# Token-major projections of 512 columns, transposed afterwards by pairs of heads, in a two-layer hybrid encoder

## The chip, the cores and the metric

The kernel runs on one core of a Trainium2 chip. The metric is device time in microseconds (us) of one execution, as the median of several runs. The core's engines work side by side, each through its own instruction list in order: TensorE (PE in the profile; its weight loads stand apart as PEld), VectorE (DVE), ScalarE (ACT), GpSimd (POOL), and the queue of SyncE (SP), which here only issues DMAs.

## The reference

The input is 256 tokens of 2048 features. Two pre-norm residual layers follow each other, then a last RMSNorm.

- Layer 0 (even) projects the normalised tokens with one matrix into eight query heads, two key heads and two value heads of branch A (grouped-query attention, RMS-normalised q and k, rotary positions), into q, k, v of branch B (eight heads of differential attention with a distance bias: two softmaxes over 64-wide halves, the second subtracted with a learned factor, then a norm per head), and into a gate of 2048 columns.
- Layer 1 (odd) projects into q, k, v and gate of sixteen heads (branch C). Its three dilated windows are merged by their softmax denominators, which for 256 tokens is one softmax with a bias and a mask.

```
proj = einsum('bsd,de->bse', rms_norm(h, g), w_in)
y    = concat(attention outputs) * silu(gate)
h    = h + einsum('bse,ed->bsd', y, w_out)
```

Inputs and outputs are float32.

## The kernel before

Every large product is done in a split form. A weight group of 1024 columns by 128 rows is loaded as `raw` (512 KB, SP's queue, four buffers), ACT copies it to `hi` (rounded to fp32r), DVE subtracts to get `lo`; activations are held as such a pair too. A product is hi·hi + hi·lo + lo·hi, three passes of TensorE. Both split instructions are issued with high priority (lines 160, 161), so each projection carries, beside its matmuls, one ACT and one DVE instruction of 1024 columns per group.

A projection of the 256 tokens is one of two kinds of job:

- `job_t` (lines 168 to 170, through `mm3`) is token-major: the stationary operand is 128 tokens of the activations, the moving one 512 weight columns. 512 output columns take 2 token tiles x 16 feature tiles x 3 passes = 96 matmuls of 512 columns. Its result has tokens on the partitions.
- `job_e` (lines 199, 200) is feature-major: the stationary operand is 128 weight columns, the moving one is hi and lo of all 256 tokens, 512 columns wide, for the weight's `hi`, and hi alone, 256 wide, for its `lo`. 256 output columns take 2 x 16 pairs of such matmuls, 64 in all. Its result has features on the partitions, as attention wants q and k; ACT and DVE then add its two halves (lines 203, 204).

Before, A's q, k and v, every v and the output projections are `job_t`; all gates, B's q and k, and C's q and k are `job_e`: 16 jobs of 256 columns in the even layer, 24 in the odd one. A's q and k, token-major because of their norm and rotation, are turned by four transposes of 128x128 per pair of heads (`zt`, line 527). A norm factor per token that a feature-major result needs along its free axis is made by `token_stats` with a diagonal and four small matmuls (`bps`, line 240), once per layer.

A head's attention is: scores (6 matmuls of 256 columns, in B 8, into a PSUM tile `bank`), a bias on DVE, row maximum on DVE, exponential on ACT, scaling on ACT, four transposes of the softmax (line 346), a split of those, the values' product (6 matmuls of 256 columns), the gate. Branch B then transposes the result for its norm (line 417), takes a power on POOL (line 221) and spreads the factor over the partitions with two more matmuls (`rb`, line 421).

The order of each engine's list is set at compile time by the framework's scheduler, which goes through the program in the order in which it is written and lets later matmuls pass where earlier ones are not ready by its own estimate. On the chip each engine keeps that list. There are four PSUM tiles `acc` (two per job) and four `att` (attention, `zt`, `bps`).

Of the kernel before, what the change touches and what calls it, by code (L numbers as in the profile page):

```python
# [17 lines left out]
P = 128  # L18
# [46 lines left out]
def job_columns(name):  # L65

    if name == "even":
        cols = [(A_KV0, 512)]
        for g in range(4):
            c = g * 256  # L70
            cols += [(c, 512)] * (g % 2 == 0) + [(GATE_E + c, 256), (GATE_E + 1024 + c, 256), (B_Q0 + c, 256), (B_K0 + c, 256)]
            cols += [(B_V0 + c, 512)] * (g % 2 == 0)
        return cols
    if name == "odd":
        cols = []
        for g in range(8):
            c = g * 256
            cols += [(3 * D + c, 256), (c, 256)]
            if g % 2 == 0:
                cols.append((2 * D + c, 512))  # L80
            cols.append((D + c, 256))
        return cols
    return list(CHUNKS_E if name == "out_even" else CHUNKS)
# [19 lines left out]
def trunk(ctx, tc, x, xt, w_even, w_oe, w_odd, w_oo, gain_cols, rows, final_g, rope_c, geo_c, out):  # L103
# [81 lines left out]
    def job_e(w, c0, wd, a):  # L185


        kn = 1024 // wd
        ps = [acc.tile([P, 512], F32, tag="acc", name=f"acc_e{b}") for b in range(wd // P)]
        for kg in range(NK // kn):  # L190
            hi, lo = wgroup(w, c0, wd, kg)
            for b in range(wd // P):
                for kk in range(kn):
                    k = kg * kn + kk
                    bs = slice(b * P, (b + 1) * P)
                    whole = (ps[b], hi[:, kk, bs], a[k].rearrange("p i s -> p (i s)"))
                    half = (ps[b][:, :S], lo[:, kk, bs], a[k][:, 0])
                    first, second = (whole, half) if k == 0 else (half, whole)
# [6 lines left out]
        return [e[:, b] for b in range(2)]  # L205

# [21 lines left out]
    def token_stats(parts, scale):  # L228

        ss = small.tile([P, NT], F32, tag="ss", name="ss")  # L230
        V.reduce_sum(ss, parts, axis=AX.X)
        rstd = small.tile([P, NT], F32, tag="rstd", name="rstd", bufs=2)
        V.tensor_copy(rstd, rsqrt_mean(ss, D, NORM_EPS, NT))
        rs = small.tile([P, NT], F32, tag="rs", name="rs", bufs=2)
        V.tensor_scalar_mul(rs, rstd, scale)
        ps = att.tile([P, 512], F32, tag="att", name="bps")
        for t in range(NT):
            diag = work.tile([P, S], F32, tag="yf", name="diag")[:, :P]
            V.tensor_scalar_mul(diag, ident, rstd[:, t:t + 1])
            T.matmul(ps[:, t * P:(t + 1) * P], ones, diag, start=True, stop=True)  # L240
        bc = heads.tile([P, S], F32, tag="bc", name="bc", bufs=1)
        V.tensor_copy(bc, ps[:, :S])
        return rstd, rs, bc
# [6 lines left out]
    def evac_q(ps, n=2):  # L250
        t = heads.tile([P, 2, 2, S], F32R, tag="q", name="q", bufs=2)
        for b in range(n):
            split(t[:, b, 0], t[:, b, 1], ps[b])
        return t

    def evac_k(ps, bc):
        t = heads.tile([P, 2, 2, S], F32R, tag="k", name="k", bufs=2)
        kf = work.tile([P, 2, S], F32, tag="kf", name="kf")
        for b in range(2):
            V.tensor_mul(kf[:, b], ps[b], bc)  # L260
        split(t[:, :, 0], t[:, :, 1], kf)
        return t
# [3 lines left out]
    def evac_q64(ps):  # L266
        t = heads.tile([P, 2, 2, S], F32R, tag="q", name="q", bufs=2)
        for b in range(2):
            for j in range(2):
                js, other = slice(64 * j, 64 * j + 64), slice(64 - 64 * j, 128 - 64 * j)  # L270
                A.activation(t[js, b, j], ps[b][js], AF.Copy)
                V.tensor_sub(t[other, b, j], ps[b][js], f(t[js, b, j]))
        return t

    def evac_k64(ps, bc):
        kh = heads.tile([P, 2, 2, S], F32R, tag="k", name="kh", bufs=2)
        kl = heads.tile([P, 2, 2, S], F32R, tag="k", name="kl", bufs=2)
        kf = work.tile([P, 2, S], F32, tag="kf", name="kf")
        for b in range(2):
            V.tensor_mul(kf[:, b], ps[b], bc)  # L280
        for j in range(2):
            js, other = slice(64 * j, 64 * j + 64), slice(64 - 64 * j, 128 - 64 * j)
            A.activation(kh[js, :, j], kf[js], AF.Copy)
            A.activation(kh[other, :, j], kf[js], AF.Copy)
            V.tensor_sub(kl[js, :, j], kf[js], f(kh[js, :, j]))
            A.activation(kl[other, :, j], f(kl[js, :, j]), AF.Copy)
# [12 lines left out]

    def evac_gate(ps, bc):  # L300

        gt = heads.tile([P, 2, S], F32, tag="gate", name="gate", bufs=2)
        for b in range(2):
            V.tensor_mul(gt[:, b], ps[b], bc)
        e = work.tile([P, 2, S], F32, tag="e", name="e", bufs=1)
        A.activation(e, gt, AF.Exp, scale=-1.0)
        V.tensor_scalar_add(e, e, 1.0)
        for b in range(2):
            for c in range(0, S, S // 4):
                V.reciprocal(e[:, b, c:c + S // 4], e[:, b, c:c + S // 4])  # L310
        V.tensor_mul(gt, gt, e)
        return gt
# [62 lines left out]
    def biased(sp, rs, bias):  # L375
        s = stile()
        for t in range(NT):
            V.scalar_tensor_tensor(s[:, t], sp[:, t], rs[:, t:t + 1], bias[:, t], op0=ALU.mult, op1=ALU.add)  # L378
        return s
# [8 lines left out]
    def head_b(h, i, q, kh, kl, v, vs, gate, rs):  # L388
        bias = alibi(2.0 ** -(i + 1), False)
        es, rd = [], []  # L390
        ps = [bank(), bank()]
        for j in range(2):
            for t in range(NT):
                o, qs = ps[j][:, t * S:(t + 1) * S], q[:, j, t * P:(t + 1) * P]
                T.matmul(o, qs, kh[:, j], start=t == 0, stop=False)  # L395
                T.matmul(o, qs, kl[:, j], start=False, stop=t == NT - 1)  # L396
            sp = ps[j].rearrange("p (t k) -> p t k", t=NT)
            s = biased(sp, rs, bias)
# [4 lines left out]
        for t in range(NT):  # L403
            A.activation(p[:, t], p[:, t], AF.Copy, scale=rd[0][:, t:t + 1])
            V.scalar_tensor_tensor(p[:, t], e2[:, t], rd[1][:, t:t + 1], p[:, t], op0=ALU.mult, op1=ALU.add)
        ph, pl = transposed(p, ps[0])
# [18 lines left out]
    def head_c(h, q, k, v, vs, gate, rs):  # L425
        bias = alibi(float(np.exp2(np.float32(-8.0 * (h + 1) / 16))), True)
        ps = bank()
        sp = scores(ps, q[:, 0], q[:, 1], k[:, 0], k[:, 1])
        p = biased(sp, rs, bias)
# [3 lines left out]
        weighted_v(h, p, v, vs, gate, ps)  # L433
# [64 lines left out]
    def tok_heads(ps, i, c0=0):  # L498

        z = work.tile([P, NT, 2 * HD], F32, tag="z", name="z", bufs=3)  # L500
        for t in range(NT):
            A.activation(z[:, t], ps[t][:, c0:c0 + 2 * HD], AF.Copy, scale=rstd[:, t:t + 1])
        sq = work.tile([P, 512], F32, tag="sq", name="sq", bufs=1)
        A.activation(sq, z.rearrange("p t c -> p (t c)"), AF.Square)
        ss = small.tile([P, 4], F32, tag="ss4", name="ss4")
        V.reduce_sum(ss, sq.rearrange("p (n e) -> p n e", e=HD), axis=AX.X)
        r = rsqrt_mean(ss, HD, NORM_EPS, 4, "ra")
        z3 = z.rearrange("p t (n e) -> p (t n) e", n=2)
        V.tensor_mul(z3, z3, r.unsqueeze(2).to_broadcast([P, 4, HD]))
        t2 = work.tile([P, NT, 2 * HD], F32, tag="t2", name="t2", bufs=1)  # L510
        for t in range(NT):
            s5 = z[:, t].rearrange("p (n s h e) -> p n s h e", n=2, s=2, h=2)
            o5 = t2[:, t].rearrange("p (n s h e) -> p n s h e", n=2, s=2, h=2)
            tab = rq[:, i, t, 1].rearrange("p (s h e) -> p s h e", s=2, h=2)
            for hh in range(2):
                V.tensor_mul(o5[:, :, :, hh], s5[:, :, :, 1 - hh],
                             tab[:, :, hh].unsqueeze(1).to_broadcast([P, 2, 2, 32]))
        z4 = z.rearrange("p t (n e) -> p t n e", n=2)
        V.tensor_mul(z4, z4, rq[:, i, :, 0].unsqueeze(2).to_broadcast([P, NT, 2, HD]))
        V.tensor_add(z, z, t2)  # L520
        return z

    def pair_t(z, tag):
        ps = att.tile([P, 512], F32, tag="att", name="zt")
        for j in range(2):
            for t in range(NT):
                T.transpose(ps[:, j * S + t * P:j * S + (t + 1) * P], z[:, t, j * HD:(j + 1) * HD], ident)
        dst = heads.tile([P, 2, 2, S], F32R, tag=tag, name=tag, bufs=1 if tag == "ka" else 2)
        split(dst[:, :, 0], dst[:, :, 1], ps.rearrange("p (j k) -> p j k", j=2))
        return dst  # L530

    rstd, rs_b, bc = token_stats(parts, 1.0 / math.sqrt(64))
# [137 lines left out]
```

## Time and profile before

| | before |
|---|---|
| median of 3 runs | 914.29 us (914.02 to 914.72) |
| profiled execution, time | 914.34 us |
| its span, first to last instruction | 912.6 us |
| PE busy | 901.6 us, 99% |
| DVE busy | 677.8 us, 74% |
| ACT busy | 528.6 us, 58% |
| mean granted TensorE clock | 0.998 of full speed |
| DMA, mean | 180 GB/s, 50.8% of 16 engines in the main queue |

Busy time of PE counts an instruction from its start to a modelled end, so neighbours overlap; what a matmul really takes of the engine is the distance from its start to the next one's. The chain is the work that ended last, followed back from the end, and tells by which engine and line the span was filled.

### The profile page before, as it was taken

To read this page: it belongs to the slowest core of one execution; us is meant where nothing else is said; L and a number is where in the kernel's file an instruction comes from. 1 tells how busy PE (TensorE), PEld (TensorE's weight loads), DVE (VectorE), ACT (ScalarE), POOL (GpSimd) and SP (SyncE) were. 2 spreads that over 40 slices of the span, in tenths; PEclk is the share of its full clock that TensorE was granted. 3 is DMA by queue.
4 is the path that set the end of the run, shared out by engine and by line. 5 is a ranking of instruction groups with operands and counts; after the bars stand their busy time and mean duration, and the time that the engine had idled before them with its cause. 6 is when DMAs were issued, how large, how long until landed. Compare 5 with 4: busy or idle time off the path is not lost.

```text
span 912.6 us, 13324 instructions
## 1 busy us (share of the span) xinstructions
PE 901.6 (99%) x4928; PEld 778.0 (85%) x4928; DVE 677.8 (74%) x1089; ACT 528.6 (58%) x909; POOL 87.0 (10%) x69
## 2 busy tenths in 40 slices
PE   9999999999999999999999999999999999999996
PEld 7888888888888887788888888888888888888886
DVE  6699788877979877656746886687758685776663
ACT  7756667575577666555445665465546464555551
POOL 0010010020200002000001120022003110202000
PEclk9999999999999999999999999999999999999999
DMA  8854544544544444455554445544454445456552
GB/s 327 316 211 150 186 171 151 175 162 162 191 159 177 145 178 165 138 190 186 179 195 170 170 161 188 186 164 167 174 191 160 181 166 184 162 185 215 188 192 95
DMA packets 47041, 164.46 MB, mean 180 GB/s; under 512 B 5376, under 2 KB 6144, under 8 KB 46976
## 3 DMA queue, kind: packets, MB, share of 16 engines
q1 hardware_dynamic: 46656, 162.57, 50.8%
q0 software_dynamic: 320, 1.05, 0.5%
q8 instruction: 38, 0.62, 0.3%
q14 instruction: 27, 0.22, 0.1%
HBM read 161.50 MB, written 2.10 MB: 179 GB/s over the span
## 4 chain that ended last, share of the span: by engine, by line
PE 96%; DVE 1%; DMA 1%; issue 1%; SPq 0%; ACT 0%; POOLq 0%; POOL 0%; DVEq 0%; ACTq 0%
PE acc_e L200 32%; PE acc_e L199 18%; PE acc_t L169 13%; PE acc_t L168 13%; PE acc_t L170 13%; PE bank L346 2%; PE bank L170 1%; PE bank L168 1%; PE bank L169 1%; DMA xk<-in_xt 1%; PE bank L326 1%; PE bank L325 1%; PE bank L324 1%; PE bank L396 0%; PE bank L395 0%
## 5 line engine op out<-in xcount | busy, mean ns | idle before, releaser
L161 DVE TENSOR_TENSOR lo<-raw,hi 128x1024 fp32r<-128x1024 f32 (+1 forms) x294 | 365.5, 1244 | 179.4 <-ACT hi L160 179.0
L160 ACT ACTIVATE hi<-raw 128x1024 fp32r<-128x1024 f32 (+1 forms) x294 | 309.6, 1054 | 285.8 <-PE acc_t L170 117.3
L200 PE MATMUL acc_e<-u,hi 128*128 128x512 f32 x1200 | 432.1, 399 | 0.0
L199 PE MATMUL acc_e<-u,lo 128*128 128x256 f32 x1200 | 338.5, 282 | 0.0
L200 PEld LDWEIGHTS acc_e<-u,hi 128*128 128x128 f32 x1200 | 225.4, 188 | 46.5
L199 PEld LDWEIGHTS acc_e<-u,lo 128*128 128x128 f32 x1200 | 226.7, 189 | 4.4
L169 PE MATMUL acc_t<-lo,u 128*128 128x512 f32 x288 | 111.7, 394 | 0.0
L170 PE MATMUL acc_t<-hi,u 128*128 128x512 f32 x288 | 110.7, 390 | 0.0
L168 PE MATMUL acc_t<-hi,u 128*128 128x512 f32 x288 | 102.7, 393 | 0.4 <-ACT u L214 0.4
L169 PE MATMUL acc_t<-lo,y 128*128 128x512 f32 (+1 forms) x256 | 96.6, 379 | 0.5 <-DVE lo L161 0.5
L383 POOL TENSOR_SCALAR bias<-geo 128x512 f32<-128x512 f32 x24 | 44.9, 1870 | 541.3 <-DVE s L378 520.4
L170 PE MATMUL acc_t<-hi,y 128*128 128x512 f32 (+1 forms) x256 | 95.2, 377 | 0.0
L168 PE MATMUL acc_t<-hi,y 128*128 128x512 f32 (+1 forms) x256 | 89.0, 379 | 0.6 <-ACT y L247 0.6
L169 PEld LDWEIGHTS acc_t<-lo,u 128*128 128x128 f32 x288 | 54.3, 189 | 11.3 <-DVE lo L161 0.4
L168 PEld LDWEIGHTS acc_t<-hi,u 128*128 128x128 f32 x288 | 53.8, 189 | 11.7 <-ACT u L214 1.1
L170 PEld LDWEIGHTS acc_t<-hi,u 128*128 128x128 f32 x288 | 54.2, 188 | 10.9
L310 DVE RECIPROCAL e<-e 128x64 f32<-128x64 f32 x128 | 56.3, 504 | 0.4
L169 PEld LDWEIGHTS acc_t<-lo,y 128*128 128x128 f32 x256 | 48.2, 188 | 9.5 <-DVE lo L161 1.0
L168 PEld LDWEIGHTS acc_t<-hi,y 128*128 128x128 f32 x256 | 47.7, 188 | 9.3 <-ACT y L247 0.8
L170 PEld LDWEIGHTS acc_t<-hi,y 128*128 128x128 f32 x256 | 48.2, 188 | 8.3
L203 ACT ACTIVATE sum<-acc_e 128x256 f32<-128x256 f32 x80 | 30.0, 375 | 20.3 <-PE acc_e L200 19.6
L204 DVE TENSOR_TENSOR sum<-acc_e,sum 128x256 f32<-128x256 f32 x80 | 33.2, 415 | 0.4 <-ACT sum L203 0.3
(155 smaller groups left out, 923.0 us busy)
## 6 DMA issues: line engine op xcount, KB each, us to landing
raw<-in_w_in_odd SPq DMA_DIRECT2D x128, 512.0 KB, 3.2
raw<-in_w_in_even SPq DMA_DIRECT2D x102, 512.0 KB, 3.2
raw<-in_w_out_even SPq DMA_DIRECT2D x32, 512.0 KB, 3.2
raw<-in_w_out_odd SPq DMA_DIRECT2D x32, 512.0 KB, 3.7
tok<-in_x SPq DMA_DIRECT2D x4, 512.0 KB, 8.6
xk<-in_xt SPq DMA_DIRECT2D x6, 256.0 KB, 6.9
raw<-in_w_in_even SPq DMA_DIRECT2D x4, 256.0 KB, 4.0
gf<-in_final_norm_g POOLq DMA_DIRECT2D x4, 256.0 KB, 4.4
```

What stands on the lines that cost most here:

```text
L160: A.activation(hi[:, ks], rv[:, ks], AF.Copy)
L161: splits.append(V.tensor_sub(lo[:, ks], rv[:, ks], f(hi[:, ks])))
L168: T.matmul(ps, ah, bh, start=start, stop=False)
L169: T.matmul(ps, ah, bl, start=False, stop=False)
L170: T.matmul(ps, al, bh, start=False, stop=stop)
L199: T.matmul(*first, start=k == 0, stop=False)
L200: T.matmul(*second, start=False, stop=k == NK - 1)
L203: A.activation(e[:, b], ps[b][:, S:], AF.Copy)
L204: V.tensor_add(e[:, b], ps[b][:, :S], e[:, b])
L310: V.reciprocal(e[:, b, c:c + S // 4], e[:, b, c:c + S // 4])
L346: T.transpose(ps[:, kt * S + t * P:kt * S + (t + 1) * P], p[:, t, kt * P:(kt + 1) * P], ident)
L383: G.tensor_scalar_mul(b, geo[:, 0], -slope)
```

## The change

All `job_e` are gone. The gates, B's q and k, and C's q and k become `job_t` of 512 columns, 20 in number, where 40 `job_e` of 256 stood. ACT evacuates each with the token's factor as a scale (`evac_t`); a gate becomes z·(1 + tanh z) with z half the projection (`gate_t`), in place of exponential, addition and reciprocal. Queries, keys and gates are then turned by pairs of heads: four transposes of 128x128 into one PSUM tile (`turned`), then the split or, for a gate, one copy. In each group of four heads the softmaxes come before the V projection and the values' products after it. `token_stats` loses its diagonal and its matmuls; the bias is added with one DVE instruction per head in place of two, the factor being in q and k already.

```diff
-    def job_e(w, c0, wd, a):
...
-                    T.matmul(*first, start=k == 0, stop=False)
-                    T.matmul(*second, start=False, stop=k == NK - 1)
-        e = work.tile([P, 2, S], F32, tag="kf", name="sum")
-        for b in range(2):
-            A.activation(e[:, b], ps[b][:, S:], AF.Copy)
-            V.tensor_add(e[:, b], ps[b][:, :S], e[:, b])
...
-            T.matmul(ps[:, t * P:(t + 1) * P], ones, diag, start=True, stop=True)
...
+    def evac_t(ps, r):
+        z = work.tile([P, NT, 512], F32, tag="z", name="z", bufs=3)
+        for t in range(NT):
+            A.activation(z[:, t], ps[t], AF.Copy, scale=r[:, t:t + 1])
+        return z
+    def gate_t(ps, rh):
+        z = evac_t(ps, rh)
+        for t in range(NT):
+            th = work.tile([P, 512], F32, tag="th", name="th", bufs=1)
+            A.activation(th, z[:, t], AF.Tanh)
+            V.scalar_tensor_tensor(z[:, t], th, 1.0, z[:, t], op0=ALU.add, op1=ALU.mult)
+        return z
+    def turned(z, pair):
+        ps = att.tile([P, 512], F32, tag="att", name="zt")
+        for j in range(2):
+            for t in range(NT):
+                c = (2 * pair + j) * HD
+                T.transpose(ps[:, j * S + t * P:j * S + (t + 1) * P], z[:, t, c:c + HD], ident)
+        return ps.rearrange("p (j k) -> p j k", j=2)
...
-        for b in range(2):
-            for c in range(0, S, S // 4):
-                V.reciprocal(e[:, b, c:c + S // 4], e[:, b, c:c + S // 4])
...
-        ps = job_e(w_odd, 3 * D + c, 256, u)
...
-        q = evac_q(job_e(w_odd, c, 256, u))
...
-        k = evac_k(job_e(w_odd, D + c, 256, u), bc)
-        for j in range(2):
-            head_c(2 * g + j, q[:, j], k[:, j], v[:, g % 2], slice(j * HD, j * HD + HD), gate[:, j], rs)
+        zg = gate_t(ps, rh)
+        zq = evac_t(job_t(w_odd, c, 512, u), rs)
+        zk = evac_t(job_t(w_odd, D + c, 512, u), rstd)
+        p = []
+        for pair in range(2):
+            q = pair_t(zq, pair, "q")
+            k = pair_t(zk, pair, "k")
+            p += [softmax_c(4 * g + 2 * pair + j, q[:, j], k[:, j]) for j in range(2)]
+        v = v_tile()
+        evac_v(v, job_t(w_odd, 2 * D + c, 512, u), rstd)
+        for pair in range(2):
+            gate = pair_gate(zg, pair)
+            for j in range(2):
+                weighted_v(4 * g + 2 * pair + j, p[2 * pair + j], v[:, pair], slice(j * HD, j * HD + HD), gate[:, j], bank())
```

On TensorE, in the middle of a projection of the odd layer, this stood before (`acc_e` is the PSUM tile of a `job_e`, `u,lo` and `u,hi` its activations with the weight part):

```order
L199 MATMUL acc_e_5060<-u,lo 128x256
L200 MATMUL acc_e_5060<-u,hi 128x512
L199 MATMUL acc_e_5060<-u,lo 128x256
L200 MATMUL acc_e_5060<-u,hi 128x512
L199 MATMUL acc_e_5060<-u,lo 128x256
```

In the changed kernel the V projection of the odd layer's second group reads like this (`acc_t` is the PSUM tile of a `job_t`; `zt` the tile of `turned`, here of a pair of keys):

```order
L159 MATMUL acc_t_5400<-hi,u 128x512 [waits Activation_49]
L159 MATMUL acc_t_5401<-hi,u 128x512
L234 MATMUL zt<-ident,z 128x128 [waits Activation_49]
L234 MATMUL zt<-ident,z 128x128 x2
L160 MATMUL acc_t_5400<-lo,u 128x512 [waits DVE_49]
L161 MATMUL acc_t_5400<-hi,u 128x512
L159 MATMUL acc_t_5400<-hi,u 128x512
```

Alternating widths have become one width, and transposes that wait for ACT's evacuation stand between the matmuls of the next job.

The second place is TensorE's list at the start of the even layer's output projection, where the last heads of branch B end. Before (`rb` spreads a head's norm factor; `y` is a head's finished output, the stationary operand of the output projection):

```order
L170 MATMUL acc_t_3872<-hi,y 128x512
L421 MATMUL bank<-ident,rb 128x128 [waits Pool_49]
L421 MATMUL bank<-ident,rb 128x128
L421 MATMUL bank<-ident,rb 128x128 [waits Activation_49,Pool_49]
L421 MATMUL bank<-ident,rb 128x128
L168 MATMUL acc_t_3699<-hi,y 128x512 [waits Activation_49]
L169 MATMUL acc_t_3699<-lo,y 128x512
```

In the changed kernel (`s` is a softmax; line 159 stands for 168, 392 for 421):

```order
L161 MATMUL bank<-ph,v 128x256
L392 MATMUL bank<-ident,rb 128x128 [waits Pool_49]
L392 MATMUL bank<-ident,rb 128x128
L392 MATMUL bank<-ident,rb 128x128 [waits Activation_49,Pool_49]
L392 MATMUL bank<-ident,rb 128x128
L159 MATMUL acc_t_3491<-hi,y 128x512 [waits Activation_49]
L159 MATMUL acc_t_3492<-hi,y 128x512
L315 MATMUL bank<-ident,s 128x128 [waits DVE_49]
L315 MATMUL bank<-ident,s 128x128 x3
L159 MATMUL acc_t_3319<-hi,y 128x512 [waits Activation_49]
```

Two heads ended there before; now four do, and two further sets of `rb` follow later in the same two output jobs.

## Rows read from the trace of the kernel before

**Rows 1.** The page: chain that ended last, by engine, then by line.

```profile
PE 96%; DVE 1%; DMA 1%; issue 1%; SPq 0%; ACT 0%; POOLq 0%; POOL 0%; DVEq 0%; ACTq 0%
PE acc_e L200 32%; PE acc_e L199 18%; PE acc_t L169 13%; PE acc_t L168 13%; PE acc_t L170 13%; PE bank L346 2%; PE bank L170 1%; PE bank L168 1%; PE bank L169 1%; DMA xk<-in_xt 1%; PE bank L326 1%; PE bank L325 1%; PE bank L324 1%; PE bank L396 0%; PE bank L395 0%
```

**Rows 2.** PE's waits in the span: us in total, times, longest.

```profile
PE acc_t L168 <- ACT y L247: 0.6, 1, 0.6
PE acc_t L169 <- DVE lo L161: 0.5, 1, 0.5
PE acc_t L168 <- ACT u L214: 0.4, 1, 0.4
PE bank L421 <- POOL rb L221: 0.2, 1, 0.2
```

**Rows 3.** Windows from job start to job start: length, PE busy (x instructions), clock, DMA.

```profile
450.53:472.29 21.76, 21.76 (x97) 1.00 0.62 216
472.29:483.59 11.30, 11.30 (x66) 1.00 0.53 188
```

**Rows 4.** Timeline, PE: start, length of one matmul; `job_e`, then `job_t`.

```profile
100.41 0.28 PE L199 MATMUL acc_e<-u,lo 128*128 128x256 f32 x1
100.52 0.40 PE L200 MATMUL acc_e<-u,hi 128*128 128x512 f32 x1
100.76 0.28 PE L199 MATMUL acc_e<-u,lo 128*128 128x256 f32 x1
101.93 0.40 PE L168 MATMUL acc_t<-hi,u 128*128 128x512 f32 x1
102.16 0.39 PE L169 MATMUL acc_t<-lo,u 128*128 128x512 f32 x1
```

**Rows 5.** Windows as in rows 3: jobs that hold attention matmuls or transposes.

```profile
483.59:496.32 12.73, 12.73 (x77) 1.00 0.49 177
496.32:508.05 11.73, 11.73 (x69) 1.00 0.39 137
508.05:521.06 13.01, 13.01 (x81) 1.00 0.54 190
63.05:76.15 13.10, 13.10 (x82) 1.00 0.48 162
472.29:569.28 96.99, 96.99 (x545) 1.00 0.49 174
```

**Rows 6.** Windows as in rows 3: `job_t` that hold attention matmuls or transposes.

```profile
29.17:51.43 22.26, 22.26 (x102) 1.00 0.75 271
403.99:426.64 22.65, 22.65 (x105) 1.00 0.54 187
545.51:569.28 23.77, 23.77 (x113) 1.00 0.54 191
```

**Rows 7.** Groups by line: busy us, mean ns of one, idle before.

```profile
L310 DVE RECIPROCAL e<-e 128x64 f32<-128x64 f32 x128 | 56.3, 504 | 0.4
L204 DVE TENSOR_TENSOR sum<-acc_e,sum 128x256 f32<-128x256 f32 x80 | 33.2, 415 | 0.4 <-ACT sum L203 0.3
L203 ACT ACTIVATE sum<-acc_e 128x256 f32<-128x256 f32 x80 | 30.0, 375 | 20.3 <-PE acc_e L200 19.6
L294 ACT ACTIVATE v<-acc_t,rstd 128x512 fp32r<-128x512 f32 x12 | 8.2, 681 | 3.2 <-PE acc_t L170 3.2
```

**Rows 8.** Timeline, DVE, then PE: A's first keys ready, then turned.

```profile
52.29 0.67 DVE L520 TENSOR_TENSOR z<-z,t 128x512 f32<-128x512 f32 x1
56.36 0.60 PE L527 MATMUL zt<-ident,z 128*128 128x128 f32 x4
```

**Rows 9.** Timeline, start of the even output projection: branch B's last norm.

```profile
370.43 0.27 PE L417 MATMUL bank<-ident,on 128*128 128x128 f32 x1
373.47 0.43 PE L421 MATMUL bank<-ident,rb 128*128 128x128 f32 x2 [0.23 <-POOL rb L221]
374.47 0.49 PE L168 MATMUL acc_t<-hi,y 128*128 128x512 f32 x1 [0.57 <-ACT y L247]
```

More of the change, by code (lines that the diff above doesn't have):

```diff
@@ L68, in job_columns @@
         cols = [(A_KV0, 512)]
[L69 to L72, printed above, removed]
+        for c in (0, 512):
+            cols += [(b + c, 512) for b in (0, GATE_E, GATE_E + 1024, B_Q0, B_K0, B_V0)]
         return cols
     if name == "odd":
[L75 to L82, printed above, removed]
+        return [(b * D + c, 512) for c in range(0, D, 512) for b in (3, 0, 1, 2)]
     return list(CHUNKS_E if name == "out_even" else CHUNKS)
@@ L231, in token_stats @@
         V.reduce_sum(ss, parts, axis=AX.X)
[L232 to L239, printed above, removed]
-            T.matmul(ps[:, t * P:(t + 1) * P], ones, diag, start=True, stop=True)
-        bc = heads.tile([P, S], F32, tag="bc", name="bc", bufs=1)
-        V.tensor_copy(bc, ps[:, :S])
-        return rstd, rs, bc
+        r3 = small.tile([P, 3, NT], F32, tag="rstd", name="rstd", bufs=2)
+        V.tensor_copy(r3[:, 0], rsqrt_mean(ss, D, NORM_EPS, NT))
+        V.tensor_scalar_mul(r3[:, 1], r3[:, 0], scale)
+        V.tensor_scalar_mul(r3[:, 2], r3[:, 0], 0.5)
+        return r3[:, 0], r3[:, 1], r3[:, 2]
     def split(hi, lo, src):
@@ new lines, in turned, with pair_t @@
+    def turned(z, pair):
[5 more added lines that the diff above has]
+        return ps.rearrange("p (j k) -> p j k", j=2)
+    def pair_t(z, pair, tag, bufs=2):
+        ps = turned(z, pair)
+        dst = heads.tile([P, 2, 2, S], F32R, tag=tag, name=tag, bufs=bufs)
+        split(dst[:, :, 0], dst[:, :, 1], ps)
+        return dst
@@ L251, in evac_q, with pair_gate, pair_q64 @@
+    def pair_gate(z, pair):
+        ps = turned(z, pair)
+        gt = heads.tile([P, 2, S], F32, tag="gate", name="gate", bufs=3)
+        A.copy(gt, ps)
+        return gt
+    def pair_q64(z, pair):
+        ps = turned(z, pair)
         t = heads.tile([P, 2, 2, S], F32R, tag="q", name="q", bufs=2)
-        for b in range(n):
-            split(t[:, b, 0], t[:, b, 1], ps[b])
-        return t
-    def evac_k(ps, bc):
-        t = heads.tile([P, 2, 2, S], F32R, tag="k", name="k", bufs=2)
-        kf = work.tile([P, 2, S], F32, tag="kf", name="kf")
-        for b in range(2):
-            V.tensor_mul(kf[:, b], ps[b], bc)
-        split(t[:, :, 0], t[:, :, 1], kf)
-        return t
@@ L266, in evac_q64 @@
-    def evac_q64(ps):
-        t = heads.tile([P, 2, 2, S], F32R, tag="q", name="q", bufs=2)
-        for b in range(2):
-            for j in range(2):
[L270 to L275, printed above, removed]
+        for j in range(2):
+            js, other = slice(64 * j, 64 * j + 64), slice(64 - 64 * j, 128 - 64 * j)
+            A.activation(t[js, :, j], ps[js], AF.Copy)
+            V.tensor_sub(t[other, :, j], ps[js], f(t[js, :, j]))
@@ L276, in evac_k64, with pair_k64 @@
+        return t
+    def pair_k64(z, pair):
+        ps = turned(z, pair)
         kh = heads.tile([P, 2, 2, S], F32R, tag="k", name="kh", bufs=2)
         kl = heads.tile([P, 2, 2, S], F32R, tag="k", name="kl", bufs=2)
-        kf = work.tile([P, 2, S], F32, tag="kf", name="kf")
-        for b in range(2):
-            V.tensor_mul(kf[:, b], ps[b], bc)
         for j in range(2):
             js, other = slice(64 * j, 64 * j + 64), slice(64 - 64 * j, 128 - 64 * j)
-            A.activation(kh[js, :, j], kf[js], AF.Copy)
-            A.activation(kh[other, :, j], kf[js], AF.Copy)
-            V.tensor_sub(kl[js, :, j], kf[js], f(kh[js, :, j]))
+            A.activation(kh[js, :, j], ps[js], AF.Copy)
+            A.activation(kh[other, :, j], ps[js], AF.Copy)
+            V.tensor_sub(kl[js, :, j], ps[js], f(kh[js, :, j]))
@@ L373, in head_a, with biased @@
         weighted_v(h, p, v, vs, gate, ps)
-    def biased(sp, rs, bias):
+    def biased(sp, bias):
         s = stile()
-        for t in range(NT):
-            V.scalar_tensor_tensor(s[:, t], sp[:, t], rs[:, t:t + 1], bias[:, t], op0=ALU.mult, op1=ALU.add)
+        V.tensor_add(s, sp, bias)
         return s
@@ L405, in head_b @@
             V.scalar_tensor_tensor(p[:, t], e2[:, t], rd[1][:, t:t + 1], p[:, t], op0=ALU.mult, op1=ALU.add)
+        return p
+    def head_b(h, p, v, vs, gate):
+        ps = [bank(), bank()]
         ph, pl = transposed(p, ps[0])
@@ L516, in tok_heads @@
                 V.tensor_mul(o5[:, :, :, hh], s5[:, :, :, 1 - hh],
[L517 to L520, printed above, removed]
-        return z
[L523 to L530, printed above, removed]
@@ L532, in trunk @@
-    rstd, rs_b, bc = token_stats(parts, 1.0 / math.sqrt(64))
+                             tab[:, :, hh].unsqueeze(1).to_broadcast([P, n, 2, 32]))
+            V.tensor_mul(z3, z3, rq[:, i, t, 0].unsqueeze(1).to_broadcast([P, n, HD]))
+            V.tensor_add(z[:, t], z[:, t], t2)
+        return z
+    rstd, rs, rh = token_stats(parts, 1.0 / math.sqrt(64))
     v_a = v_tile("va", 1)
     evac_v(v_a, ps_kv, rstd, 256)
-    k_a = pair_t(tok_heads(ps_kv, 1), "ka")
-    for g in range(4):
-        half, c = g // 2, g * 256
-        if g % 2 == 0:
-            ps = job_t(w_even, c, 512, u) if g else ps_q0
-            zs = [tok_heads(ps, 0, i * 256) for i in range(2)]
-        q = pair_t(zs[g % 2], "q")
-        gate = evac_gate(job_e(w_even, GATE_E + c, 256, u), bc)
-        for j in range(2):
-            head_a(2 * g + j, q[:, j], k_a[:, half], v_a[:, 0], slice(half * HD, half * HD + HD), gate[:, j])
-        gate = evac_gate(job_e(w_even, GATE_E + 1024 + c, 256, u), bc)
-        q = evac_q64(job_e(w_even, B_Q0 + c, 256, u))
-        kh, kl = evac_k64(job_e(w_even, B_K0 + c, 256, u), bc)
-        if g % 2 == 0:
-            v = v_tile()
-            evac_v(v, job_t(w_even, B_V0 + c, 512, u), rstd)
-        for j in range(2):
-            head_b(8 + 2 * g + j, 2 * g + j, q[:, j], kh[:, j], kl[:, j], v[:, g % 2], slice(j * HD, j * HD + HD), gate[:, j], rs_b)
@@ new lines, in trunk @@
+    k_a = pair_t(tok_heads(ps_kv, 1, 2), 0, "ka", 1)
+    for g in range(2):
+        c = 512 * g
+        zq = tok_heads(job_t(w_even, c, 512, u) if g else ps_q0, 0, 4)
+        zg = gate_t(job_t(w_even, GATE_E + c, 512, u), rh)
+        for pair in range(2):
+            q = pair_t(zq, pair, "q")
+            gate = pair_gate(zg, pair)
+            for j in range(2):
+                head_a(4 * g + 2 * pair + j, q[:, j], k_a[:, g], v_a[:, 0], slice(g * HD, g * HD + HD), gate[:, j])
+        zg = gate_t(job_t(w_even, GATE_E + 1024 + c, 512, u), rh)
+        zq = evac_t(job_t(w_even, B_Q0 + c, 512, u), rs)
+        zk = evac_t(job_t(w_even, B_K0 + c, 512, u), rstd)
+        v = v_tile()
+        ps = []
+        for pair in range(2):
+            q = pair_q64(zq, pair)
+            kh, kl = pair_k64(zk, pair)
+            ps += [softmax_b(4 * g + 2 * pair + j, q[:, j], kh[:, j], kl[:, j]) for j in range(2)]
+        evac_v(v, job_t(w_even, B_V0 + c, 512, u), rstd)
+        for pair in range(2):
+            gate = pair_gate(zg, pair)
+            for j in range(2):
+                head_b(8 + 4 * g + 2 * pair + j, ps[2 * pair + j], v[:, pair], slice(j * HD, j * HD + HD), gate[:, j])
@@ L571, in trunk @@
             square_sum(parts_o[:, t, i:i + 1], tok[:, t, cs])
[L574 to L588 removed]
+    for g in range(4):
+        c = 512 * g
+        ps = job_t(w_odd, 3 * D + c, 512, u)
+        if g == 0:
+            rstd, rs, rh = token_stats(parts_o, 1.0 / math.sqrt(HD))
+        zg = gate_t(ps, rh)
+        zq = evac_t(job_t(w_odd, c, 512, u), rs)
+        zk = evac_t(job_t(w_odd, D + c, 512, u), rstd)
+        p = []
+        for pair in range(2):
+            q = pair_t(zq, pair, "q")
+            k = pair_t(zk, pair, "k")
+            p += [softmax_c(4 * g + 2 * pair + j, q[:, j], k[:, j]) for j in range(2)]
+        v = v_tile()
+        evac_v(v, job_t(w_odd, 2 * D + c, 512, u), rstd)
+        for pair in range(2):
+            gate = pair_gate(zg, pair)
+            for j in range(2):
+                weighted_v(4 * g + 2 * pair + j, p[2 * pair + j], v[:, pair], slice(j * HD, j * HD + HD), gate[:, j], bank())
     parts = small.tile([P, NT, 5], F32, tag="parts5", name="parts5", bufs=1)
```

78 lines of the change are left out of this document (21 added, 57 removed).

## The prediction, as it was put on record

> **What bounds the kernel now.** I read the chain first: 96% of the span is PE, half of it the two lines of `job_e` [rows 1]. The reader should see that no other engine has more than 1% there. Then PE's waits: in the whole main part it waits four times, 1.7 us in all [rows 2]; 0.4 of that is at the start, and 1.3 us lie where the even layer's output projection begins. So time is PE's own work, and the question is what a matmul costs from its start to the next one's. The page's mean durations don't tell that, since neighbours overlap; windows that reach from the first matmul of a job to the first of the next do. Their counts hold one or two instructions too many, those in flight at an edge.
>
> A quiet `job_t` of 512 columns takes 21.76 us for 96 matmuls, 0.227 each; a quiet `job_e` of 256 columns takes 11.30 us for 64, 0.353 per pair [rows 3]. The timeline shows how: a 512-wide matmul is followed after 0.23 or 0.24 us, a 256-wide one after 0.11 [rows 4]. Two `job_e` are thus 22.60 us where one `job_t` would be 21.76.
>
> **The change part by part.** All sums are of the profiled execution, 914.34 us, span 912.6 and 1.7 us around it, which I leave as they are; it stands 0.05 us above the median of 914.29, so the sum is taken over to the median unchanged.
>
> *Projections.* 40 `job_e` go, 20 `job_t` come. I need the mean `job_e`. From the inserted work in rows 5: twelve 256-wide attention matmuls add 12.73 - 11.30 = 1.43 us (0.119 each), four transposes 11.73 - 11.30 = 0.43 (0.11 each), so a head of branch C is worth 1.86. The odd layer's period of 96.99 us holds six `job_e`, one V job and four heads: (96.99 - 21.76 - 4 x 1.86) / 6 = 11.30. In the even layer the job of 13.10 us holds twelve such matmuls and four transposes: 13.10 - 1.86 = 11.24; the cheapest I find is 13.01 - 1.86 = 11.15 [rows 5]. I take 11.20 for the 16 even jobs and 11.29 for the 24 odd ones: 179.2 + 271.0 = 450.2. Against that 20 x 21.76 = 435.2 [rows 3]. Gain 15.0 us; at 11.15 throughout it is 10.8, at 11.30 it is 16.8.
>
> The rows show 0.227 us for 512 columns and 0.353 for 512 + 256 [rows 3]. Here the Trainium skill speaks against the change. Its page "TensorE: Matmul & The Clock Gate" (section "Wait — 56ns, not 53.3ns?") puts the distance at columns divided by 2.4 GHz plus about 2.5 ns, by which both kinds of job, with the same 49,152 columns per 512 outputs, would differ by 0.08 us only and the term be 1.6 us instead of 15.0. The measured distances decide, and they lie above that rule by 11 ns for a 512-wide matmul and by more for a pair.
>
> *Transposes.* 24 pairs of heads in the odd layer (queries, keys, gates) and 16 new ones in the even layer (A's gates, B's queries, keys, gates) are turned: 40 x 4 = 160 transposes. Four in a `job_e` cost 0.43 [rows 5]. In a `job_t`, where all will now stand, eight cost 22.65 - 21.76 = 0.89, or 0.445 per four, and four small matmuls (the `bps`) 22.26 - 21.76 = 0.50 [rows 6]. I take 0.47, between the two of the same kind of job: 40 x 0.47 = 18.8 us added; bounds 17.2 and 20.0.
>
> *The factor's broadcast.* The `bps` matmuls go, twice 0.50: 1.0 us less [rows 6].
>
> *Attention inside other jobs.* A head and its four transposes inside a `job_t` cost 23.77 - 21.76 = 2.01, against 1.86 in `job_e` [rows 5, 6]: 0.15 more. Some 24 of the 32 heads move from the one to the other; bounds 0 and 3.6. The eight transposes at 0.89 show hardly any surcharge, so I take a third, 1.2 us.
>
> *Waits.* The 0.5 us for `lo` [rows 2] come from a DVE queue that held a split back. DVE loses reciprocals and half sums, 56.3 + 33.2 us [rows 7], and more small ones, so I take these 0.5 away. The other 0.8 us (ACT `y`, POOL `rb`) are of a chain that stays; bounds -1.3 and a rival below.
>
> *What is at nothing.* ACT loses 30.0 us of half sums [rows 7] and the exponentials of the gates; it gains 40 evacuations of 512 columns at 0.68 us, taken from the same operation on v [rows 7], that is 27 us, the tanh and the gates' copies: about even, and PE's work hides it with ACT idle 42% of the span. Tanh isn't in the trace; if it cost double an ordinary instruction that would be some 10 us of ACT's idle time, and if its result came late, only the gate, wanted a job later, would be. DMA moves the same 512 KB groups, at half the engines' time [rows 5]; SP's order changes with the jobs, and each group is used as fast as before within 4%. Before a first turning the chain of norm and rotation is longer (four heads at once), but a whole `job_t` of 21.76 us covers it, and in the trace A's first keys were ready at 52.96 and turned at 56.36 [rows 8], 3.4 us to spare. If that cover is gone, each of the two turnings of A's queries could hold PE, in its strict order, for one or two us.
>
> Sum: -15.0 + 18.8 - 1.0 + 1.2 - 0.5 = +3.5, so 914.3 + 3.5 = 917.8 us. With all bounds one way, -16.8 + 17.2 - 1.0 + 0 - 1.3 = -1.9, or 912.4; the other way, without new waits, -10.8 + 20.0 - 1.0 + 3.6 = +11.8, or 926.1. The terms are worked out apart from each other, so I take 914.5 to 921 as this case's own range.
>
> **The rivals.**
>
> *A burst of heads at the even layer's end.* PE's list goes strictly in order. From a head's transposed result to the spread of its norm factor the chain takes 373.47 - 370.43 = 3.04 us over ACT, DVE and POOL, and from there 1.0 us to the matmul that wants `y`; PE stood idle 0.23 and 0.57 us in it, once for two heads [rows 9]. Now four heads end there, with three sets of `rb`, and behind each stand the output projection's matmuls, the only work left. The eight norms of branch B are spread over two such places. If five more sets stall for 0.8 us each, that is 4.0 on top: 921.8. For it: the scheduler places an instruction when it believes it ready, and here it was late on the chip. Against it: two output jobs are interleaved as cover, and softmaxes are now done earlier. It decides from about 3 us of PE waiting for POOL `rb` and ACT `y`.
>
> *Uniform width takes inserted work for less.* The other side. One `job_e` took twelve attention matmuls and four transposes for 13.01 - 11.30 = 1.71 us where the sum of the parts is 1.86 [rows 5]. If it is the break of the 512/256 alternation that makes inserts dear, a stream of one width would have all 24 heads at 1.71, 3.6 us less, and the transposes at 0.43: -15.0 + 17.2 - 1.0 - 3.6 - 0.5 = -2.9, or 911.4. Against it stands the one clean case in a `job_t`, at 2.01 [rows 6]. It decides if a V job with a head in it falls under 23.5 us.
>
> *The terms cancel.* With `job_e` at 11.30 throughout and transposes at 0.43: -16.8 + 17.2 - 1.0 + 1.2 - 0.5 = +0.1, or 914.4. For it: both prices are in rows 3 and 5; against it: the even layer's jobs are cheaper, and no turning will stand in a `job_e`.
>
> *Columns alone bind.* If equal columns cost equal time, the first term is nothing: 18.8 - 1.0 + 1.2 - 0.5 = +18.5, or 932.8. Rows 3 are against it. The Trainium skill's page "TensorE: Matmul & The Clock Gate", by its rule given above, would make it 1.6 us less than that.
>
> **How the numbers follow.** My forecast has 0.54, the burst 0.18, the uniform width 0.10, the cancelling 0.15, columns alone 0.03. A measurement of this kernel can tell a change of about 0.2%, 1.8 us, from none: faster is below 912.5, slower above 916.1. Faster holds the uniform width and a little of the low corner: 0.11. Same holds the cancelling and that fifth of my forecast's range that lies under 916.1: 0.27. Slower has the rest, 0.62. The range of 8 in 10 runs from 912.4, the favourable corner, to 923.5, a little over the burst; columns alone and the unfavourable corner stay outside.
>
> **What would show it.** A quiet `job_t` still at 21.76 us and 0.227 per matmul; four transposes between them at 0.45 to 0.50; an odd period of 4 x 21.76 + 4 x 1.86 to 2.01 + 6 x 0.47, that is 97.3 to 97.9 us against 96.99; PE's waits under 2 us in all; DVE's busy time down by more than 100 us with no effect. I am wrong if the odd period falls below 96.5, if the transposes cost under 0.35 or over 0.6 per four, or if PE's waits list grows beyond 3 us, in particular at the first turning of A's queries or where branch B ends.

## The result and the profile after

The changed kernel takes 919.69 us (median of 4 runs, 919.38 to 919.99), the kernel before beside it 914.50: a ratio of 1.0055, 95% interval 1.0038 to 1.0073. It is slower by 5.2 us, where +3.5 was forecast; 919.69 lies in the forecast's own range of 914.5 to 921. The profiled execution took 919.56 us with a span of 917.8, again 5.2 us more than before.

The page of the kernel after, first its busy times (share of the span, instructions), then the chain that ended last, by engine and by line:

```profile
PE 907.0 (99%) x4440; PEld 760.4 (83%) x4440; DVE 559.6 (61%) x751; ACT 532.6 (58%) x866; POOL 78.2 (9%) x67
...
PE 96%; ACT 1%; issue 1%; DMA 1%; SPq 0%; DVE 0%; POOLq 0%; POOL 0%; DVEq 0%; ACTq 0%
PE acc_t L160 29%; PE acc_t L161 29%; PE acc_t L159 29%; PE zt L234 2%; PE bank L315 1%; PE bank L159 1%; PE bank L161 1%; PE bank L160 1%; DMA raw<-in_w_in_even 1%; PE bank L294 1%; PE bank L295 1%; PE bank L293 1%; ACT hi L151 0%; PE bank L363 0%; PE bank L364 0%
```

The path is still TensorE's [rows 1]: the two lines of `job_e` have become three of one kind, and the turnings (`zt`) are now 2% of it. DVE lost 118 us of busy time and ACT gained 4; the chain holds 0% of the one and 1% of the other.

Windows of the kernel after, as in [rows 3, 5, 6]: a quiet job; a job with four transposes; one with eight (the first odd projection, with transposes of the even layer's result); the two jobs that hold the attention of four heads; one period of the odd layer.

```profile
452.66:474.42 21.76, 21.76 (x97) 1.00 0.55 194
474.42:496.71 22.29, 22.29 (x102) 1.00 0.55 189
430.01:452.66 22.65, 22.65 (x105) 1.00 0.54 186
496.71:523.61 26.90, 26.90 (x142) 1.00 0.45 157
523.61:550.27 26.66, 26.66 (x140) 1.00 0.47 158
474.42:572.03 97.61, 97.61 (x474) 1.00 0.50 173
```

The reader should compare three of them with before. The quiet `job_t` is the same 21.76 us to the hundredth. The odd period is 97.61 us against 96.99 [rows 5], inside the 97.3 to 97.9 that the prediction gave. The odd layer's first projection starts at 430.01 us, where it started at 426.64 before [rows 6]: 3.4 of the 5.2 us arise up to there, 1.8 behind it (four periods at +0.62, less 0.5 for the `bps`).

TensorE's waits after (us in total, times, longest):

```profile
PE idle L130 <- POOL ones L120: 1.0, 1, 1.0
PE acc_t L159 <- ACT hi L151: 0.6, 1, 0.6
PE acc_t L159 <- ACT u L183: 0.4, 2, 0.2
PE bank L388 <- ACT on L383: 0.3, 1, 0.3
PE bank L159 <- ACT ph L209: 0.2, 1, 0.2
```

1.1 us lie in the main part, against 1.3 before [rows 2], again all at the start of the even output projection. But they are other waits: `lo` and the norm's factor no longer hold TensorE. All three are now ACT's, which had 0.6 us of them before. The chain there, in order of time (start, us, what), shows whose queue it has become:

```profile
347.15 1.06 ACT hi L151
348.20 0.49 ACT ph L209
348.69 0.98 ACT s L304 x4
349.67 0.32 ACT on L383
349.99 0.04 issue
350.04 0.33 PE bank L388
350.36 0.45 PE zt L234 x4
350.81 0.02 issue
350.84 0.39 ACT gate L246
...
351.73 0.68 ACT s L304 x3
352.41 0.80 ACT s L371 x2
353.21 0.97 ACT hi L151
```

From 347 to 354 us nearly every step is ACT's: exponentials (L304), scaling (L371), evacuations and the copy of a turned gate (L246, new) stand one behind the other, with weight splits (L151) between.

### The profile page after: what moved, and what is told of

The parts are those of the page before. It is cut to its first block, busy times and chain, and to the rows that moved or that the text cites. A ratio compares the mean times of both kernels' runs of the same rounds, so it can differ in the third digit from the quotient of the medians.

```text
span 917.8 us, 11973 instructions
## 1 busy us (share of the span) xinstructions
PE 907.0 (99%) x4440; PEld 760.4 (83%) x4440; DVE 559.6 (61%) x751; ACT 532.6 (58%) x866; POOL 78.2 (9%) x67
## 4 chain that ended last, share of the span: by engine, by line
PE 96%; ACT 1%; issue 1%; DMA 1%; SPq 0%; DVE 0%; POOLq 0%; POOL 0%; DVEq 0%; ACTq 0%
PE acc_t L160 29%; PE acc_t L161 29%; PE acc_t L159 29%; PE zt L234 2%; PE bank L315 1%; PE bank L159 1%; PE bank L161 1%; PE bank L160 1%; DMA raw<-in_w_in_even 1%; PE bank L294 1%; PE bank L295 1%; PE bank L293 1%; ACT hi L151 0%; PE bank L363 0%; PE bank L364 0%
## 5 line engine op out<-in xcount | busy, mean ns | idle before, releaser
L151 ACT ACTIVATE hi<-raw 128x1024 fp32r<-128x1024 f32 (+1 forms) x294 | 309.4, 1054 | 307.7 <-PE acc_t L161 292.0
L160 PE MATMUL acc_t<-lo,u 128*128 128x512 f32 x928 | 364.9, 395 | 0.1
L161 PE MATMUL acc_t<-hi,u 128*128 128x512 f32 x928 | 362.2, 392 | 0.0
L159 PE MATMUL acc_t<-hi,u 128*128 128x512 f32 x928 | 338.4, 393 | 0.4 <-ACT u L183 0.4
L160 PEld LDWEIGHTS acc_t<-lo,u 128*128 128x128 f32 x928 | 174.6, 188 | 36.2 <-DVE lo L152 0.6
L159 PEld LDWEIGHTS acc_t<-hi,u 128*128 128x128 f32 x928 | 174.0, 188 | 36.1 <-ACT u L183 1.2
L161 PEld LDWEIGHTS acc_t<-hi,u 128*128 128x128 f32 x928 | 174.5, 188 | 33.9
L304 ACT ACTIVATE s<-s,nm 128x256 f32<-128x256 f32 x64 | 31.7, 497 | 4.4 <-DVE nm L301 4.3
L216 ACT ACTIVATE z<-acc_t,rstd 128x512 f32<-128x512 f32 x40 | 27.2, 680 | 9.0 <-PE acc_t L161 9.0
L234 PE MATMUL zt<-ident,z 128*128 128x128 f32 x180 | 29.7, 272 | 0.0
L234 PEld LDWEIGHTS zt<-ident,z 128*128 128x128 f32 x180 | 22.4, 140 | 5.0
L346 DVE TENSOR_TENSOR s<-bank,bias 128x512 f32<-128x512 f32 x32 | 21.7, 682 | 6.9 <-POOL bias L353 4.4
L353 POOL TENSOR_TENSOR bias<-bias,geo 128x512 f32<-128x512 f32 x16 | 23.8, 1490 | 1.3
```

The source lines that it names most:

```text
L151: A.activation(hi[:, ks], rv[:, ks], AF.Copy)
L159: T.matmul(ps, ah, bh, start=start, stop=False)
L160: T.matmul(ps, ah, bl, start=False, stop=False)
L161: T.matmul(ps, al, bh, start=False, stop=stop)
L216: A.activation(z[:, t], ps[t], AF.Copy, scale=r[:, t:t + 1])
L304: A.activation(e[:, t], s[:, t], AF.Exp, bias=nm[:, t:t + 1], accum_out=den[:, t:t + 1])
```

## The experiments

All were run beside the kernel before (914.6 to 914.7 us there). My theory: the time is TensorE's work, the projections gain about 15 us and 160 exposed transposes take more than that back. The rivals: new waits at the bursts of heads; equal columns, equal time; alternation of widths as what makes `job_e` dear.

**no_turn: the new transposes left out.** The new callers of `turned` get a slice of the evacuated tile, so a turning goes with all that hangs on it: its four transposes, its PSUM tile and TensorE's wait for the evacuation.

```diff
+        if not real:
+            return z[:, :, pair * 256:pair * 256 + 256]
         ps = att.tile([P, 512], F32, tag="att", name="zt")
```

> The changed kernel without its 160 new transposes: gates, B's queries and keys and C's queries and keys are read untransposed out of the evacuated tile, so the output is not the reference's; every other instruction stays. If TensorE's own work sets the time and four transposes cost 0.47 us of it, 40 x 0.47 = 18.8 us go: 919.7 - 18.8 = 900.9, some 13.5 us under the kernel before, which is what the projections alone gain. If instead the change is slower by new waits at the bursts of four heads, with the transposes beside other work, little goes: above 914. If equal columns cost equal time (the projections gain nothing), the time is that of before, 914.

Measured: 899.89 us, ratio to before 0.9842 (0.9827 to 0.9858). The turnings cost 19.8 us and the rest of the change gains 14.7. New waits apart from the turnings, or equal columns at equal time, are out as the cause. Windows of this kernel, one odd period and two quiet jobs in it, show the same by stage:

```profile
444.07:538.89 94.82, 94.82 (x450) 1.00 0.53 178
444.07:465.83 21.76, 21.76 (x97) 1.00 0.60 194
465.83:487.59 21.76, 21.76 (x97) 1.00 0.56 194
```

Against 97.61 with transposes, an odd period pays 2.79 us for six turnings, 0.465 each. Up to the odd layer, this kernel is 8.6 us ahead of the one after (its first odd projection starts at 421.42 us, that of the kernel after at 430.01): 16 turnings, 0.54 each.

**turn_twice: each new transpose done twice.**

```diff
+                for _ in range(2 if twice else 1):
+                    T.transpose(ps[...], z[:, t, c:c + HD], ident)
```

> The changed kernel with each of its 160 new transposes done twice into the same place; nothing else is changed. If they are fully on the path at 0.44 to 0.47 us per four (0.44 where eight stand together), 17.6 to 18.8 us are added: 937.3 to 938.5. If half of them stand beside waits of TensorE, 9 us: 929. If waits rule, the same 919.7 within 2 us.

Measured: 937.86 us, 18.2 more than the kernel after; ratio to before 1.0254 (1.0240 to 1.0268). The second set costs 0.455 us per four, as forecast, so none of it is hidden. Two windows of this kernel, from its second job to the odd layer and one odd period, show that the price is the same in both layers:

```profile
30.12:438.26 408.14, 406.39 (x2013) 1.00 0.52 170
482.68:582.97 100.29, 100.29 (x497) 1.00 0.52 168
```

The odd period is 2.68 us longer than the 97.61 of the kernel after, 0.447 per turning. The even layer is 7.25 us longer than the 400.89 of the same stretch after (29.12 to 430.01), 0.453 for each of 16. Its waits at the even output projection are 1.5 us, against 1.1.

**turn_r: the transposes in fp32r.** `z` is written as fp32r and turned with an fp32r identity.

```diff
-        z = work.tile([P, NT, 512], F32, tag="z", name="z", bufs=3)
+        z = work.tile([P, NT, 512], F32R, tag="z", name="z", bufs=3)
...
+                T.transpose(pr[:, j * S + t * P:j * S + (t + 1) * P], z[:, t, c:c + HD], ident_r if r else ident)
```

> The changed kernel with the evacuated tiles of gates, B's and C's queries and keys held as fp32r and transposed as fp32r with an fp32r identity (the values are rounded once more). If a 128-wide fp32 transpose costs 0.11 us because it is two passes, an fp32r one is about half: four of them 0.22 to 0.28 in place of 0.47, 40 x 0.19 to 0.25 = 7.6 to 10 us less, 909.7 to 912.1, faster than the kernel before. If its cost is a fixed one of a short matmul with its weight load, the time stays at 919.7.

Measured: 916.40 us, ratio to before 1.0020 (1.0011 to 1.0028): 3.3 us less than after, under half of the 7.6 to 10 expected. A job with four such transposes and one odd period, in windows of this kernel:

```profile
473.02:495.25 22.23, 22.23 (x102) 1.00 0.55 189
473.02:570.14 97.12, 97.12 (x474) 1.00 0.52 174
```

The job is 0.47 us over a quiet one, against 0.53 in fp32. Over the period a turning costs (97.12 - 94.82) / 6 = 0.38 us, against 0.465. Most of a short transpose's price is thus not the type of its data. What else it is, a fixed part of each matmul or its weight load, these runs don't separate.

**v_first: the change's third part undone.** The V projection stands before the softmaxes, each values' product follows its softmax at once, and queries and keys are turned pair by pair behind the V projection. The cut shows the odd layer; the even one is edited in the same way.

```diff
+        v = v_tile()
+        evac_v(v, job_t(w_odd, 2 * D + c, 512, u), rstd)
         zk = evac_t(job_t(w_odd, D + c, 512, u), rstd)
...
+                p = softmax_c(4 * g + 2 * pair + j, q[:, j], k[:, j])
+                weighted_v(4 * g + 2 * pair + j, p, v[:, pair], slice(j * HD, j * HD + HD), gate[:, j], bank())
```

> The changed kernel with its third part undone: the V projection stands before the softmaxes (in the odd layer before the K projection, as in the kernel before), and each head's values' product follows its own softmax at once. The work is the same, only its order differs. If the order is worth nothing because TensorE is filled either way, 919.7 within 1.5 us. If putting the V projection between softmax and product saved waits, they come back where no projection is left as cover, at the start of the two output projections: 4 heads, 2 to 6 us more, 922 to 926. If the deferral is itself what made the change slower, it is faster: 915 to 917.

Measured: 941.93 us, ratio to before 1.0296 (1.0282 to 1.0310): 22.2 us slower than after, far more than any theory gave. Two windows of this kernel, at the starts of the even and of the odd output projection, and TensorE's waits in the first of them:

```profile
328.45:402.64 74.19, 63.34 (x299) 0.98 0.34 114
830.57:887.77 57.20, 54.80 (x273) 1.00 0.52 166
```

```profile
PE acc_t L159 <- ACT hi L151: 2.6, 4, 0.9
PE bank L315 <- DVE s L372: 1.8, 2, 1.5
PE acc_t L159 <- ACT y L209: 1.7, 2, 1.0
PE bank L160 <- DVE pl L210: 1.1, 1, 1.1
PE acc_t L160 <- DVE lo L152: 1.0, 2, 0.5
PE bank L388 <- ACT sq L195: 0.9, 1, 0.9
```

TensorE is idle for 10.9 us of the first window and 2.4 of the second. The kernel after is idle for 1.2 us in these places. The waits listed are of the softmax chain (`s`, `pl`), of the norm (`y`, `sq`) and for weight splits (`hi`, `lo`), which stand in the same lists of ACT and DVE. Further inside the odd layer the same order costs nothing:

```profile
635.23:732.90 97.67, 97.67 (x474) 1.00 0.51 173
```

That period is 97.67 us against 97.61 after: there a next projection stands behind the heads. At the even layer's end the granted clock fell as well. This timeline of TensorE (start, length, idle before) shows matmuls at nearly twice their distance of 0.227 us, 0.43, after a stretch of waits:

```profile
390.18 0.39 PE L160 MATMUL bank<-pl,v 128*128 128x256 f32 x1 [1.13 <-DVE pl L210]
...
392.53 0.80 PE L159 MATMUL acc_t<-hi,y 128*128 128x512 f32 x1 [0.70 <-ACT y L209]
393.12 0.63 PE L160 MATMUL acc_t<-lo,y 128*128 128x512 f32 x1
393.55 0.63 PE L159 MATMUL acc_t<-hi,y 128*128 128x512 f32 x1
```

In the trace the clock stood at its lower level, 1.2 GHz, for 3.4 us there (the window's mean is 0.98), which is worth some 1.7 us by estimate. About 1.6 us of the difference to the kernel after arose in the first 31 us, before any edited work. That part may be the execution's own: TensorE's waits for `u` at the start are 0.4 us in the traces of before and after and 1.9 in that of regroup_tanh, where no edit touches the start either. With the 12 us of idle time that makes some 15 of the 23.1 us between the two profiled executions; the rest was not taken apart. So the rival of the burst named the right place. Its chain is only a part of what waits there: `y` and `rb` hold 2.3 of the 10.9 us. That the V projection as cover keeps the rest away is what this run speaks for; the edit also moves the turnings, and the two were not tried apart.

**regroup: `job_e` of the kernel before, matmuls grouped by width.**

```diff
-                    first, second = (whole, half) if k == 0 else (half, whole)
...
+                steps = whole + half if kg == 0 or (b == 1 and kg < NK // kn - 1) else half + whole
+                for n, m in enumerate(steps):
+                    T.matmul(*m, start=kg == 0 and n == 0, stop=kg == NK // kn - 1 and n == len(steps) - 1)
```

> The kernel before with each feature-major projection's matmuls grouped by width: of one weight group and one 128-column block, the four 512-wide ones together and the four 256-wide ones together, in place of alternating. The sums are the same. If the alternation is what makes a pair cost 0.353 us, it falls to 0.227 + 0.120 = 0.347, 40 jobs x 32 pairs x 0.006 = 7.7 us less: about 907. If a pair costs 0.353 in any order, 914.5 stays. If the column-wise grouping makes the low halves' lateness visible, it is slower than 914.5.

Measured: 911.92 us, ratio 0.9971 (0.9961 to 0.9982). It is faster than both kernels, by about a third of the 7.7 us. A quiet `job_e` of it, one with twelve matmuls of scores, and one with a values' product and four transposes:

```profile
471.57:482.71 11.14, 11.14 (x66) 1.00 0.59 194
482.71:495.34 12.63, 12.63 (x77) 1.00 0.51 174
506.96:520.05 13.09, 13.09 (x82) 1.00 0.56 169
```

The quiet job takes 11.14 us in place of 11.30 [rows 3]: 0.16 saved of the 0.2 that the expectation's 0.006 us per pair would give. The second takes 12.63 in place of 12.73, the third 13.09 in place of 13.01 [rows 5]: jobs that hold attention gained less or lost, hence a third of the sum. Over a whole odd period (471.57 to 567.98) 0.58 us are saved. So alternation is part of why two `job_e` cost more than one `job_t`, the smaller part: 22.28 against 21.76 is left. Those are 128 matmuls against 96 for the same columns; that their number makes the rest was not tested.

**tanh_before: the kernel before with the gate by tanh.**

```diff
-        A.activation(e, gt, AF.Exp, scale=-1.0)
-        V.tensor_scalar_add(e, e, 1.0)
...
+        A.activation(e, gt, AF.Tanh, scale=0.5)
+        V.scalar_tensor_tensor(e, e, 1.0, gt, op0=ALU.add, op1=ALU.mult)
+        A.activation(gt, e, AF.Copy, scale=0.5)
```

> The kernel before with the gate's sigmoid by tanh: per pair of heads one DVE instruction in place of ten (no reciprocals) and one more on ACT; nothing else is changed. DVE loses some 60 us of busy time. If DVE is off the path except for the 0.5 us wait for lo, 914.6 stays, or 914.1. If a crowded DVE stretched the projections in the even layer by more than the waits list shows, 2 us or more go: under 912.6.

Measured: 915.45 us, ratio 1.0007 (0.9999 to 1.0016), no difference. Its busy times:

```profile
PE 902.4 (99%) x4928; PEld 777.3 (85%) x4928; DVE 621.8 (68%) x945; ACT 533.5 (58%) x925; POOL 92.4 (10%) x69
```

DVE lost 56 us of its 677.8 and the time didn't move. The wait for `lo` is gone from TensorE's list, as the prediction had it for a lighter DVE, but the time is no shorter for it: waits for `u` at the start are 1.1 us in this trace, against 0.4 [rows 2].

**regroup_tanh: both edits.** The diffs are those above.

> The kernel before with both edits: matmuls of the feature-major projections grouped by width, and the gate by tanh. If grouping is a matter of TensorE alone and DVE is off the path, the time of the grouping alone, 911.9, or 0.5 us under it. If grouping makes TensorE wait for lo more often and DVE's relief takes these waits away, 909 to 911.

Measured: 912.14 us, ratio 0.9973 (0.9963 to 0.9984): the grouping alone. That the grouping gave less than expected is no matter of DVE.

**gate_last: the grouped kernel, with branch B's gate projected between softmax and values' product.**

```diff
-        gate = evac_gate(job_e(w_even, GATE_E + 1024 + c, 256, u), bc)
         q = evac_q64(job_e(w_even, B_Q0 + c, 256, u))
...
+        p = [softmax_b(2 * g + j, q[:, j], kh[:, j], kl[:, j], rs_b) for j in range(2)]
+        gate = evac_gate(job_e(w_even, GATE_E + 1024 + c, 256, u), bc)
+        for j in range(2):
+            head_b(8 + 2 * g + j, p[j], v[:, g % 2], slice(j * HD, j * HD + HD), gate[:, j])
```

> The kernel with matmuls grouped by width, and the change's third part carried over to it in the even layer: in each group of two heads branch B's gate is projected last, between the softmaxes and the values' products, so that 11 us of projection stand over the softmax chain. The work is the same. If the waits of 1.5 to 2 us at the start of the even output projection come from that chain, most of them go: 910 to 911. If they come from the norm after the values' product (POOL, ACT), which stays where it was, 911.9 stays.

Measured: 911.63 us, ratio 0.9966 (0.9954 to 0.9978). It is the lowest median of the kernels that leave nothing out, but its interval overlaps that of the grouping alone; whether it gains anything is open. The waits have moved (`ph` 0.7 and `lo` 0.6 us in its trace, in place of 0.6 for `y` and 0.2 for `rb` in that of the grouping) and have not gone. The 1.5 to 2 us that the expectation gave them were too many.

## Why the prediction was right

*What bounds.* Right: without the transposes 19.8 us go, with twice as many 18.2 come, and 56 us of DVE work less, by themselves, change nothing (tanh_before). TensorE's own work is the time.

*Projections, broadcast, attention in other jobs.* The three terms and the relief made -15.3 us; the kernel without the new transposes is at -14.7. The price of a quiet `job_t` read from windows [rows 3] carried over to the hundredth. The missing 0.6 us show in the odd period: for three `job_t` in place of six `job_e` and three heads moved, the terms give it 96.99 - 2.46 + 0.15 = 94.68 us without turnings, no_turn has 94.82, and there are four periods. The heads are the likely place. Each costs (94.82 - 4 x 21.76) / 4 = 1.95 us in a `job_t`, where the surcharge taken, a third of 0.15 over 1.86, gives 1.91. The rule that was weighed against them, by which equal columns would have left a gain of 1.6 us, is refuted by no_turn.

*Transposes.* Forecast 18.8 us, measured 19.8. In the odd layer 0.465 us per four against 0.47: right. In the even layer 0.54: mis-sized by 1.1 us. This is the larger part of the 1.7 us that the sum fell short of. Two windows of the kernel after, then the same work in no_turn, show where it lies: from the second job to the start of B's last projection, and from there to the odd layer.

```profile
29.12:302.35 273.23, 273.23 (x1337) 1.00 0.51 177
302.35:430.01 127.66, 126.33 (x616) 1.00 0.48 165
```

```profile
29.29:297.14 267.85, 267.85 (x1293) 1.00 0.54 181
297.14:421.42 124.28, 123.33 (x593) 1.00 0.51 170
```

The first eleven turnings cost 5.38 us, 0.49 each; the last five, around the start of the output projection, 3.38 us, 0.68 each (no_turn stood 0.17 us behind at the start). The transposes' own work is not what is dearer, since turn_twice paid 0.453 for a second set in the even layer. Of the 1.0 us that the last five cost above 0.47 each, 0.4 are idle time (1.33 us against 0.95 in the second windows), and the gate's copy is one of the ACT steps of the chain there. The other 0.6 us were not taken apart. Both misses, 1.0 us here and 0.6 above, go the same way: the forecast was not right by cancelling.

*Waits.* A step that failed, though a small one: "DVE loses reciprocals and half sums ... so I take these 0.5 away". `lo` left the list, as forecast, but waits for ACT took its place, 1.1 us against 1.3, so 0.2 went; and in tanh_before a lighter DVE alone made the time no shorter.

*What was priced at nothing.* Right. The prediction gave A's first turning 3.4 us to spare [rows 8] and feared for A's queries, whose norm and rotation now take longer. Their cover held. These are the last DVE steps of their two token tiles, then the weight load and the first transpose:

```profile
63.22 0.68 DVE L489 TENSOR_TENSOR z<-z,t 128x512 f32<-128x512 f32 x1
...
67.49 0.68 DVE L489 TENSOR_TENSOR z<-z,t 128x512 f32<-128x512 f32 x1
...
67.96 0.14 PEld L234 LDWEIGHTS zt<-ident,z 128*128 128x128 f32 x1
...
68.19 0.27 PE L234 MATMUL zt<-ident,z 128*128 128x128 f32 x1
```

The weight load begins at 67.96, before the second tile is done at 68.17, so it can only need the first, done at 63.90: 4.1 us to spare. The other three transposes follow at 73.33.

*The rivals.* The burst did not come (1.1 us of waits instead of the 3 from which it would decide), though v_first shows that the place is dangerous: with the V projection ahead of the softmaxes, TensorE is idle for 13.3 us at the starts of the two output projections, most of it for other steps than the rival's `rb` and `y`. The prediction saw that "softmaxes are now done earlier" and gave it no price. Uniform width did not take inserted work for less: four transposes cost 0.465, not 0.43, and a head 1.95, not 1.71. The cancelling and the columns alone fell with no_turn.

## What to carry to other kernels

Where TensorE is the path, price a change of layout by start-to-start distances over whole jobs, from quiet windows, and set the transposes that the new layout needs against it: here projections of one width, with all else that changed, saved 14.7 us and 160 transposes took 19.8. Look first for a gain that needs no transposes: the same matmuls grouped by width were worth 2.7 us. If more heads are grouped, leave a projection between their softmaxes and the values' products, since TensorE keeps its order and a late step becomes idle time where no projection follows: v_first lost at the ends of both layers and nothing in the odd periods before.

## What the runs showed of the hardware

A 128x128 transpose costs TensorE 0.11 to 0.13 us in fp32, half of the 0.227 of a matmul with four times the columns; in fp32r it is only 0.015 to 0.02 us less (0.47 against 0.53 us per four in a job, 0.38 against 0.465 over a period). A 512-wide matmul followed by a 256-wide one costs more in alternation than grouped: 11.30 against 11.14 us per 64 in quiet jobs. POOL's power of 128x8 took 2.57 and 1.64 us in the kernel after, that of 128x2 0.70 to 0.73; TensorE waited for neither there. After waits of 0.2 to 1.1 us in close succession the granted clock fell to 1.2 GHz for 3.4 us in v_first; in the other traces it fell only behind TensorE's last matmul.
